# Four pairs of a tuned MoE kernel: inner product 2 split once more into seven small products

## The chip, the core and the metric

The kernel runs on one core of a Trainium2 chip. A core has five engines that each take their own instructions in order: TensorE (PE, matrix products; its weight loads are listed as PEld), VectorE (DVE), ScalarE (ACT), GpSimd (POOL), which here mostly issues DMAs, and SyncE (SP), which issues DMAs too. Engines wait for each other by semaphores. SBUF is the on-chip memory, PSUM the eight banks into which TensorE writes. The metric is the device time of one execution in microseconds (us); the median of the runs counts.

## The reference

A soft mixture of experts: every token goes through all eight experts, and the outputs are added, weighted by the softmax of the router's logits.

```python
# x: 16 x 512 x 512, router_logits: 16 x 512 x 8, expert_weights: 8 x 512 x 2048
probs = softmax(router_logits)
for e in range(8):
    output += probs[:, :, e:e+1] * (x @ expert_weights[e])
```

So the output is one product of a matrix of 8192 x 4096 (each token's x, scaled by each of its eight probabilities) with one of 4096 x 2048 (the experts' weights, stacked).

## The kernel before

The big product is done by a scheme of the Strassen-Winograd kind: a product of two matrices that are cut into 2 x 2 blocks is made of seven products of blocks in place of eight, at the price of sums of blocks. The first level gives seven outer products, numbered 1 to 7 here (P1 is the first). The second level cuts each again: each piece of it (a `Product`, 256 tokens by 1024 columns) is made of seven inner products, steps 1, 5, 6, 2, 7, 3, 4 (`STEPS`, L353), each of eight matmuls of 128x512 (`K8`). A `Left` holds the left operand of a piece in fp16: `t[0]`, `t[1]` (the two halves of its depth), and the sums `s2` and `i`; a `Right` holds the weights and their sums.

The pieces are run in pairs, called stages. P1 has stages 0 to 6 (`ND` = 7); its results are stored to the DRAM tensors `kept`. In a stage the two pieces take turns, step by step, in slots 0 to 13; the hooks (`at`) issue loads and other work ahead of a slot.

In stages 1 to 6 the first two steps, inner products 1 and 5 of both pieces, are split a third time (`by_thirds`, from L764 on). Both pieces have the same weights, so their two left operands stand above each other as a matrix of 256 tokens by 1024, which is cut into 2 x 2 blocks; the weights are cut likewise (`third_sums`, L178). Seven small products of four 128x256 matmuls each take the place of two full products of eight 128x512 matmuls each. The fourteen small products for steps 1 and 5 are listed in L778; (p, r) is small product r of inner product p. Their sums of left operands are made by `Thirds`.

Each small or full product leaves a result in a PSUM bank, and a copy by ScalarE or an add by VectorE takes it on:

- `bank()` (tile `ps`) has six buffers, `bank2()` (tile `pt`) two. `by_thirds` keeps both `pt` banks, one for inner product 1 and one for 5; products 1 and 4 of each go through it, and the last one, (5, 4), is copied out by ScalarE (L812).
- `Product.post_alone` (L591 on) is what follows a full step. After step 1 ScalarE copies the bank of product 1 into a second PSUM bank, `b` (L596), onto which step 2 adds its matmuls; the result is then copied to an SBUF tile `h` (L604) and stored. Steps 5 and 6 are copied to `h` (L600), and steps 7 and 3 add a bank to such an `h` on VectorE.
- `h` tiles (`hpool`, 12 buffers) hold the pieces' results until their store by POOL (L121) has landed, the four sums of `Thirds`, and a few others. A tile that needs a buffer waits until an older one is free.

The order on VectorE is the order in which the program issues its work. Work that isn't bound to a slot (a `Left`'s halves, `s2`, `i`, the sums of `Thirds`, sums of weights) is put into a first-in first-out queue with an assumed cost (`later`). `slack` (L384), called after each product, keeps two clocks, one of TensorE and one of VectorE, and issues tasks from that queue while VectorE's clock is behind TensorE's; `need` issues at once all that stands ahead of a task that a product is about to use. `evacuated` charges an add to VectorE's clock.

Besides, POOL loads and stores weights during P1: casts of the expert's weights at slots 8, 2, 0 and 9 of stages 1, 3 and 5, and the "wedge" in stages 2 to 3 and 4 to 5, three VectorE sums of weights at the start of stages 3 and 5.

Of the kernel before, what the change touches and what calls it, by code (L numbers as in the profile page):

```python
# [31 lines left out]
def kernel(  # L32
# [7 lines left out]
    nc = tc.nc  # L40
# [3 lines left out]
    ADD, SUB, MUL = mybir.AluOpType.add, mybir.AluOpType.subtract, mybir.AluOpType.mult  # L44
# [5 lines left out]
    C = H // P  # L50
# [4 lines left out]
    HQ = 256  # L55
# [21 lines left out]
    def half():  # L77
        return h_tile([P, NB], f32)
# [27 lines left out]
    def tt(o, a, b, op):  # L106
        dve(nc.vector.tensor_tensor(out=o, in0=a, in1=b, op=op))  # L107
# [15 lines left out]
    def bank():  # L123
        return psum.tile([P, NB], f32, name="ps", tag="ps")

    def bank2():
        return psum.tile([P, NB], f32, name="pt", tag="pt", bufs=2)

    def mm(ps, z, w, start, stop):
        note(nc.tensor.matmul(ps, z, w, start=start, stop=stop, skip_group_check=True))  # L130
# [9 lines left out]
    def new_z():  # L140
        return zpool.tile([P, K8, HQ], f16, name="z", tag="z")
# [217 lines left out]
    class Task:  # L359


        def __init__(self, cost, make):
            self.cost, self.make, self.done = cost, make, False
# [10 lines left out]
    def need(task):  # L374
        if task is not None and not task.done:
            flush(task)
            clock["pe"] = max(clock["pe"], clock["dve"])

    def later(cost, make, first=False):
        t = Task(cost, make)  # L380
        (queue.appendleft if first else queue.append)(t)
        return t

    def slack(slot=SLOT, lag=LAG):  # L384
        clock["dve"] = max(clock["dve"], clock["pe"])
        clock["pe"] += slot
        while queue and clock["dve"] < clock["pe"] - lag:
            queue.popleft().run()

    def evacuated(cost=0.69):  # L390
        clock["dve"] = max(clock["dve"], clock["pe"]) + cost
# [53 lines left out]
    class Left:  # L445
# [6 lines left out]
        def make(self, k):  # L452
            if self.of is not None:
                need(self.of.task[k])
            t = self.t[k] = new_z()
            times(t, k, self.xb, self.pb)
            if self.less is not None:
                u = new_u()
                times(u, k, *self.less)
                tt(t, t, u, SUB)  # L460
            if self.of is not None:
                tt(t, self.of.t[k], t, SUB)
            if self.kept is not None:
                tt(t, t, self.kept.t[:, ds(k * K8, K8), :], SUB)
# [19 lines left out]
        def op(self, p):  # L484
            need(self.task[{1: 0, 5: 0, 6: "s2", 2: 1, 4: 1, 3: "i", 7: "i"}[p]])
            if p == 6:
                return self.s2
            t, i = {1: (self.t[0], 0), 5: (self.t[0], 1), 2: (self.t[1], 0), 4: (self.t[1], 1),
                    3: (self.i, 0), 7: (self.i, 1)}[p]
            return t[:, :, ds(i * HP, HP)]  # L490
# [19 lines left out]
    class Thirds:  # L510
# [19 lines left out]
        def queue(self):  # L530
            self.a.queue_make(0)
            self.b.queue_make(0)
            self.task = later(2.76, self.make)
            for left in (self.a, self.b):
                left.queue_s2()
            for left in (self.a, self.b):
                left.queue_make(1)
# [7 lines left out]
    class Right:  # L545
# [15 lines left out]
        def op(self, p):  # L561
            need(self.task.get(p))
            return self.w[p]

    TN = {2: (0, 0), 3: (0, 1), 4: (1, 0), 7: (1, 1)}

    class Product:


        def __init__(self, right, left, sink, base=None, steps=STEPS):  # L570
            self.right, self.left, self.sink, self.base, self.steps = right, left, sink, base, steps
            self.loads, self.banks, self.o = [], {}, {}
            self.apart = False

        def step(self, p):
            b = "q" if p in (5, 3) else "b" if p == 2 else "x"
# [14 lines left out]

        def post_alone(self, p, x, q, b):
            o = self.o
            if p == 1:
                self.banks["b"] = bank()
                act(nc.scalar.copy(self.banks["b"], x))  # L596
            elif p in (5, 6):
                tn = (1, 1) if p == 5 else (0, 1)
                o[tn] = half()
                act(nc.scalar.copy(o[tn], q if p == 5 else x))  # L600
            elif p in (2, 4):
                if TN[p] not in o:
                    o[TN[p]] = half()
                act(nc.scalar.copy(o[TN[p]], b if p == 2 else x))  # L604
            else:
                evacuated()
                tt(o[TN[p]], x if p == 7 else q, o[TN[p]], ADD)

# [19 lines left out]
    ND = 7  # L628
# [28 lines left out]
    def at(stage, slot, make):  # L657
        hooks.setdefault((stage, slot), []).append(make)
# [105 lines left out]
    def by_thirds(stage):  # L764

        some = stages[stage]
        left = thirds[stage]
        cols = [ds(i * HQ, HQ) for i in range(2)]
        place, keep = {}, {}

        def at_once(what):
            if what not in place:
                t = place[what] = (bank2 if what[0] == "x" else bank)()
                if what[0] in "gh":
                    some["gh".index(what[0])].banks["x" if what[1] == 1 else "q"] = t
            return place[what]
        slot = 0
        for n, (p, r) in enumerate(((1, 1), (5, 1), (1, 5), (1, 6), (5, 6), (5, 5), (1, 2),  # L778
                                    (1, 7), (5, 7), (1, 3), (1, 4), (5, 2), (5, 3), (5, 4))):
            if n in (0, 4, 7, 11):  # L780
                for make in hooks.get((stage, slot), ()):
                    make()
                slot += 1
                if slot == 2:
                    queue_lefts(stage + 1)
                    start_loads(stage + 2)
            x = at_once(("x", p))[:, cols[0]]
            q = at_once("q")[:, cols[p // 5]] if n > 1 else None
            g = at_once(("g", p))
            if r == 1:  # L790
                keep[p] = half()
            o = q if r in (5, 3) else g[:, cols[0]] if r == 2 else x
            z, w = left.op(r, p // 5), left.weights[p][r]
            for c in range(C):
                mm(o, z[:, c, :], w[:, c, :], (r == 1 or (p, r) == (1, 5)) and c == 0, c == C - 1)
            slack(0.4375, LAG if n < 6 else 1.3)
            if r == 1:
                act(nc.scalar.copy(g[:, cols[0]], x))
            elif r == 5:
                act(nc.scalar.copy(keep[p][:, cols[1]], q))  # L800
            elif r == 6:
                act(nc.scalar.copy(keep[p][:, cols[0]], x))
            elif r == 7:
                evacuated(0.42)
                tt(at_once(("h", p))[:, cols[1]], x, keep[p][:, cols[1]], ADD)
            elif r == 3:
                evacuated(0.42)
                tt(g[:, cols[1]], q, keep[p][:, cols[0]], ADD)
                if p == 1:
                    some[0].post(1)  # L810
            elif r == 4:
                act(nc.scalar.copy(place["h", p][:, cols[0]], x))  # L812
                if p == 1:
                    some[1].post(1)
        for product in some:
            product.post(5)
        return 4

    def queue_lefts(stage):
        if stage in thirds:  # L820
            if thirds[stage].task is None:
                thirds[stage].queue()
        elif stage < len(stages):
            for p in stages[stage]:
                queue_left(p.left)

    def run(stage):
        some = stages[stage]
        for p in some:
            p.left.queue_i()  # L830
        n = by_thirds(stage) if stage in thirds else 0
        for i in range(n // 2, len(some[0].steps)):
            for p in some:
                for make in hooks.get((stage, n), ()):
                    make()
                p.step(p.steps[i])
                slack()
                p.post(p.steps[i])
                n += 1
                if n == wait_for.get(stage, 1):  # L840
                    queue_lefts(stage + 1)
                if n == late.get(stage, 1):
                    start_loads(stage + 2)
                if n == 5:
                    store_loads(stage + 1)
                if n == 7:
                    finish_loads(stage + 2)
# [283 lines left out]
    def third_at(stage, slot, of, r, p):  # L1131
        def make():
            of[p] = third_sums(right[r].w[p])
        at(stage, slot, lambda: later(2.76, make))
    third_at(ND, 5, third2, 2, 1)
    third_at(ND, 7, third2, 2, 5)
    third_at(k3, 3, third3, 3, 1)
# [96 lines left out]
```

## Time and profile before

| | us |
|---|---|
| median of three runs | 1361.7 (1361.27 to 1362.39) |
| the profiled run | 1360.91 |
| its span, first to last instruction | 1359.1 |
| one of stages 2 to 5 | 23.38 |

All times of the trace below are microseconds from the start of the span. In a timeline a line gives the start, the time from the first to the last of the merged instructions (the number of them stands after the x), the engine, the line of the program, the operation, what it writes from what it reads, the shapes, and in brackets the idle time of the engine before it with what ended it. In a group of instructions the numbers after the bar are the busy time, the mean duration of one in ns, and the idle time before them. Ends of matmuls are modelled: a matmul's listed duration is longer than the distance to the next one.

### The profile page before, as it was taken

What the parts mean: (1) busy time and instruction counts of PE and PEld (TensorE: products, weight loads), DVE (VectorE), ACT (ScalarE), POOL (GpSimd) and SP (SyncE); (2) the same over time, 40 slices, a digit from 0 to 9 for tenths busy, and PEclk for the clock granted to TensorE, in tenths of its full rate; (3) what the DMA queues carried; (4) which work ended last, traced back from release to release, by engine and by line L of the source; (5) the groups of instructions that cost most, each with busy time, mean ns of one, the idle gap of its engine ahead of it and who ended that gap; (6) DMA issues with size and microseconds to landing.
All of it is one profiled execution on the core that took longest, in us unless ns stands there. A gap on an engine that the chain in (4) does not pass through costs nothing.

```text
span 1359.1 us, 18757 instructions
## 1 busy us (share of the span) xinstructions
PE 1352.8 (100%) x6846; PEld 667.1 (49%) x6846; DVE 1133.7 (83%) x1374; ACT 261.4 (19%) x525; POOL 435.9 (32%) x667
## 2 busy tenths in 40 slices
PE   9999999999999999999999999999999999999998
PEld 4555555565544444444444444444444444556564
DVE  7877687878999888787887899988889897898884
ACT  3232423233211111111111100000000000224331
POOL 3223323333222332323312122453434443232342
PEclk9999999999999999999999999999999999999999
DMA  9899979888899999999997998999999999999997
GB/s 186 242 221 247 258 232 233 255 243 250 238 341 288 287 310 273 288 285 284 309 274 279 345 318 236 247 267 251 264 251 249 263 265 315 327 302 251 199 163 131
DMA packets 191116, 355.65 MB, mean 262 GB/s; under 512 B 53040, under 2 KB 81968, under 8 KB 186160
## 3 DMA queue, kind: packets, MB, share of 16 engines
q0 software_dynamic: 89824, 189.31, 59.6%
q1 hardware_dynamic: 97456, 139.86, 33.5%
q10 hardware_dynamic: 3744, 25.30, 4.7%
q8 instruction: 53, 0.87, 0.3%
q14 instruction: 39, 0.32, 0.1%
HBM read 210.53 MB, written 180.55 MB: 288 GB/s over the span
## 4 chain that ended last, share of the span: by engine, by line
PE 99%; DMA 0%; DVE 0%; issue 0%; POOL 0%; ACT 0%; POOLq 0%
PE ps L130 75%; PE pt L130 24%; DMA w<-in_x_dram 0%; DVE z L255 0%; POOL w L121 0%; DVE h L107 0%; ACT h L1180 0%; DVE lg L295 0%; POOLq L1218 0%
## 5 line engine op out<-in xcount | busy, mean ns | idle before, releaser
L130 PE MATMUL ps<-w,z 128*128 128x512 f16 (+1 forms) x3776 | 821.3, 374 | 0.0
L130 PEld LDWEIGHTS <-z 128*128 128x128 f16 x5264 | 515.0, 98 | 574.4
L121 POOL DMA_DIRECT2D out_dram<-h x380 | 256.7, 710 | 684.1 <-ACT h L617 269.5
L130 PE MATMUL pt<-w,z 128*128 128x512 f16 (+1 forms) x1488 | 312.7, 357 | 0.0
L107 DVE TENSOR_TENSOR z<-xT,pT 128x2048 f16<-128x2048 f16 x220 | 265.9, 1217 | 0.8 <-DMA xT<-xs 0.8
L107 DVE TENSOR_TENSOR h<-ps,h 128x512 f32<-128x512 f32 x250 | 170.2, 687 | 88.0 <-PE ps L130 67.2
L130 PE MATMUL ps<-w,d 128*128 128x512 f16 x880 | 199.1, 379 | 0.0
L604 ACT COPY h<-ps 128x512 f32<-128x512 f32 x118 | 69.2, 586 | 417.9 <-PE ps L130 385.3
L130 PEld LDWEIGHTS <-d 128*128 128x128 f16 x880 | 86.1, 98 | 99.8
L107 DVE TENSOR_TENSOR z<-z,d 128x2048 f16<-128x2048 f16 x110 | 131.8, 1216 | 0.0
L107 DVE TENSOR_TENSOR h<-pt,h 128x512 f32<-128x512 f32 x123 | 83.5, 686 | 43.3 <-PE pt L130 41.0
L107 DVE TENSOR_TENSOR w<-w 128x1024 f16<-128x1024 f16 (+2 forms) x104 | 110.2, 1075 | 1.9 <-PE ps L130 1.0
L617 ACT COPY h<-ps 128x512 f32<-128x512 f32 x50 | 29.3, 586 | 391.5 <-PE ps L130 387.1
L107 DVE TENSOR_TENSOR ps<-ps,h 128x512 f32<-128x512 f32 (+1 forms) x90 | 51.9, 579 | 28.5 <-PE ps L130 24.9
L107 DVE TENSOR_TENSOR d<-z 128x1024 f16<-128x1024 f16 x110 | 74.7, 684 | 1.1
L600 ACT COPY h<-ps 128x512 f32<-128x512 f32 x97 | 53.8, 604 | 69.4 <-PE ps L130 65.3
L121 POOL DMA_DIRECT2D kept<-h x56 | 30.6, 548 | 93.7 <-ACT h L604 52.6
L121 POOL DMA_DIRECT2D out_dram<-kept x56 | 56.9, 1058 | 11.2 <-DMA out_dram<-h 5.8
L596 ACT COPY ps<-ps 128x512 f32<-128x512 f32 x59 | 33.6, 570 | 120.7 <-PE ps L130 62.6
L107 DVE TENSOR_TENSOR ps<-pt,h 128x256 f32<-128x256 f32 x38 | 16.4, 432 | 41.5 <-PE pt L130 29.4
L107 DVE TENSOR_TENSOR h<-h 128x512 f32<-128x512 f32 (+2 forms) x69 | 45.1, 675 | 0.6 <-DMA out_dram<-h 0.4
L107 DVE TENSOR_TENSOR z<-z,u 128x2048 f16<-128x2048 f16 x36 | 44.1, 1225 | 1.2
(74 smaller groups left out, 558.6 us busy)
## 6 DMA issues: line engine op xcount, KB each, us to landing
out_dram<-h POOLq DMA_DIRECT2D x380, 256.0 KB, 7.5
pT<-p_dram SPq DMA_DIRECT2D x126, 256.0 KB, 7.7
w<-wd ACTq DMA_DIRECT2D x23, 1024.0 KB, 9.4
xT<-x SPq DMA_DIRECT2D x80, 256.0 KB, 7.7
h<-kept SPq DMA_DIRECT2D x72, 256.0 KB, 7.7
h<-out_dram SPq DMA_DIRECT2D x68, 256.0 KB, 6.7
w<-in_expert_weights_dram POOLq DMA_DIRECT2D x33, 512.0 KB, 10.3
kept<-h POOLq DMA_DIRECT2D x56, 256.0 KB, 6.0
```

The costliest lines, as they stand in the source:

```text
L107: dve(nc.vector.tensor_tensor(out=o, in0=a, in1=b, op=op))
L121: note(nc.gpsimd.dma_start(out=o, in_=i, **how))
L130: note(nc.tensor.matmul(ps, z, w, start=start, stop=stop, skip_group_check=True))
L596: act(nc.scalar.copy(self.banks["b"], x))
L600: act(nc.scalar.copy(o[tn], q if p == 5 else x))
L604: act(nc.scalar.copy(o[TN[p]], b if p == 2 else x))
L617: act(nc.scalar.copy(o[tn], b))
```

## The change

In stages 2 to 5, inner product 2 of the two pieces is split like 1 and 5. A class `Twos` makes the sums of the left operands: four VectorE sums of 128x512, in a new tile `z`, as one task with an assumed cost of 1.68 us. `by_twos` runs the fourth to ninth slot of such a stage: the seven small products 1, 5, 6, 2, 7, 3, 4 stand between the full steps 6 and 7 of the two pieces. The sums of product 2's weights are made once, in stage 1. The result of product 1 is copied to SBUF, into the piece's `h` for quarter (0, 0), instead of PSUM; when the small products are done, VectorE adds their result to it (`end`).

```diff
+    class Twos:
...
+        def make(self):
+            e0, e1 = ds(0, C), ds(C, C)
+            a, b = (left.t[1][:, :, ds(0, HP)] for left in (self.a, self.b))
+            t = new_z().rearrange("p (s c) (two t) -> p s c two t", s=2, two=2)
+            for i, (p, x, y, op) in enumerate(((5, b[:, e0], b[:, e1], ADD), (6, 5, a[:, e0], SUB),
+                                               (3, a[:, e1], 6, SUB), (7, a[:, e0], b[:, e0], SUB))):
+                self.s[p] = t[:, i // 2, :, i % 2]
+                tt(self.s[p], *(self.s[v] if isinstance(v, int) else v for v in (x, y)), op)
+        def queue(self):
+            self.task = later(1.68, self.make)
+        def op(self, r):
+            need(self.task)
+            if r in self.s:
+                return self.s[r]
+            left = self.b if r == 4 else self.a
+            return left.op(2)[:, ds(0 if r == 1 else C, C), :]
...
         def post_alone(self, p, x, q, b):
             o = self.o
-            if p == 1:
+            if p == 1 and self.two:
+                o[0, 0] = half()
+                act(nc.scalar.copy(o[0, 0], x))
+            elif p == 1:
                 self.banks["b"] = bank()
                 act(nc.scalar.copy(self.banks["b"], x))
...
+    def by_twos(stage):
+
+        some, of = stages[stage], twos[stage]
+        c0, c1 = (ds(i * HQ, HQ) for i in range(2))
+        x, q, g, h = bank2(), bank2(), bank(), bank()
+        keep = []
+
+        def small(r):
+            o = q if r in (5, 3) else g if r == 2 else x
+            o = o[:, c1 if o is q else c0]
+            z, w = of.op(r), of.weights[2][r]
+            for c in range(C):
+                mm(o, z[:, c, :], w[:, c, :], r in (1, 5) and c == 0, c == C - 1)
+            slack(0.4375)
+            if r == 1:
+                act(nc.scalar.copy(g[:, c0], x[:, c0]))
+            elif r == 5:
+                keep.append(half())
+                act(nc.scalar.copy(keep[0][:, c1], q[:, c1]))
+            elif r == 6:
+                act(nc.scalar.copy(keep[0][:, c0], x[:, c0]))
+            elif r == 7:
+                evacuated(0.42)
+                tt(h[:, c1], x[:, c0], keep[0][:, c1], ADD)
+            elif r == 3:
+                evacuated(0.42)
+                tt(g[:, c1], q[:, c1], keep[0][:, c0], ADD)
+                end(0, g)
+            elif r == 4:
+                act(nc.scalar.copy(h[:, c0], x[:, c0]))
+                end(1, h)
+
+        def end(i, of):
+            o = some[i].o[0, 0]
+            evacuated()
+            tt(o, of, o, ADD)
+            some[i].sink((0, 0), o)
+
+        def full(i, p):
+            some[i].step(p)
+            slack()
+            some[i].post(p)
+        for slot, todo in enumerate((((1,), (5,)), ((0, 6),), ((6,), (2,)), ((1, 6), (7,), (3,)), ((0, 7),), ((4,), (1, 7))), 4):
+            for make in hooks.get((stage, slot), ()):
+                make()
+            for what in todo:
+                (small if len(what) == 1 else full)(*what)
+            if slot + 1 == 5:
+                store_loads(stage + 1)
+            if slot + 1 == 7:
+                finish_loads(stage + 2)
+        return 10
...
     def run(stage):
         some = stages[stage]
+        if stage in twos:
+            twos[stage].queue()
         for p in some:
             p.left.queue_i()
         n = by_thirds(stage) if stage in thirds else 0
+        if stage in twos:
+            n = by_twos(stage)
...
+    third_at(1, 5, third, 1, 2)
+    for stage in range(2, ND - 1):
+        twos[stage] = Twos(*(p.left for p in stages[stage]), third)
+        for p in stages[stage]:
+            p.two = True
```

The program as built has 64 fewer matmuls of 128x512 and 112 more of 128x256; VectorE has 16 sums of 128x512 (fp16), 8 adds of 128x256, 8 of 128x512 and 4 weight sums of 128x1024 more; ScalarE has 16 copies of 128x256 more and 8 of 128x512 fewer. The DMAs are the same ones.

More of the change, by code (lines that the diff above doesn't have):

```diff
@@ L563, in op, with __init__ @@
             return self.w[p]
+    class Twos:
+        def __init__(self, a, b, weights):
+            self.a, self.b, self.weights, self.s, self.task = a, b, weights, {}, None
+        def make(self):
[14 more added lines that the diff above has]
+            return left.op(2)[:, ds(0 if r == 1 else C, C), :]
     TN = {2: (0, 0), 3: (0, 1), 4: (1, 0), 7: (1, 1)}
@@ L572, in __init__ @@
             self.loads, self.banks, self.o = [], {}, {}
-            self.apart = False
+            self.apart = self.two = False
         def step(self, p):
@@ L817, in by_thirds @@
         return 4
+    twos = {}
+    def by_twos(stage):
[46 more added lines that the diff above has]
+        return 10
     def queue_lefts(stage):
```

## The prediction

> **What bounds the kernel now.** I read the page first, then the waits of TensorE, then the stretches of the four changed stages.
>
> ```profile
> span 1359.1 us, 18757 instructions
> PE 1352.8 (100%) x6846; PEld 667.1 (49%) x6846; DVE 1133.7 (83%) x1374; ACT 261.4 (19%) x525; POOL 435.9 (32%) x667
> PE 99%; DMA 0%; DVE 0%; issue 0%; POOL 0%; ACT 0%; POOLq 0%
> ```
> ```profile
> PE every L89 <- DVE h L86: 1.3, 1, 1.3
> PE ps L130 <- DMA w<-in_x_dram: 0.4, 1, 0.4
> PE ps L130 <- DVE lg L295: 0.3, 1, 0.3
> ```
> ```profile
> 87.65:111.03 23.38, 23.38 (x137) 13.33 (x136) 15.11 (x20) 8.23 (x18) 7.31 (x12) 1.00 1.17 263
> 111.03:134.41 23.38, 23.38 (x137) 13.29 (x136) 17.22 (x22) 8.23 (x18) 8.92 (x15) 1.00 1.10 255
> 134.41:157.79 23.38, 23.38 (x137) 13.33 (x136) 16.38 (x22) 8.24 (x18) 7.33 (x12) 1.00 1.12 233
> 157.79:181.17 23.38, 23.38 (x137) 13.29 (x136) 17.61 (x23) 8.23 (x18) 8.52 (x15) 1.00 1.08 305
> ```
>
> TensorE is the chain (99%), and all its waits are three at the kernel's start. Of the stretches (columns: PE, PEld, DVE, ACT, POOL busy, clock, DMA share, GB/s) each is one of stages 2 to 5; S below is a stage's start. Each lasts 23.38 us with TensorE busy in all of it, so time is won only by giving TensorE fewer columns, and lost by every wait put before it. VectorE is busy 15.1 to 17.6 us of 23.38.
>
> **The change part by part: TensorE's gain.**
>
> ```profile
> 92.89 0.60 PE L130 MATMUL ps<-w,h 128*128 128x256 f16 x4
> 93.33 0.60 PE L130 MATMUL pt<-w,z 128*128 128x256 f16 x4
> 93.77 3.62 PE L130 MATMUL ps<-w,d 128*128 128x512 f16 x16
> 97.22 13.98 PE L130 MATMUL ps<-w,z 128*128 128x512 f16 x64
> 111.03 1.04 PE L130 MATMUL pt<-w,z 128*128 128x256 f16 x8
> ```
>
> From 97.22 to 111.03 are 64 full matmuls: 0.2158 us each, 1.727 for a product of eight. A small product of four 128x256 matmuls takes 0.437 (87.65 to 93.77 is 14 of them). Per stage the two full products 2 (3.453) become seven small ones (3.06): -0.39, over four stages -1.57 us. That is the most this change can gain, 0.12%.
>
> **The wait before small product 5.** The new code takes both two-buffer banks of by_thirds (pt) at once. Small 1 gets the one free early; small 5 gets the one that the last small product of by_thirds, (5,4), has just filled and ScalarE must copy out first. Only small 1 stands between.
>
> ```profile
> 92.74 0.57 ACT L596 COPY ps<-ps 128x512 f32<-128x512 f32 x1 [1.90 <-DVE ps L107]
> 93.23 0.36 ACT L812 COPY ps<-pt 128x256 f32<-128x256 f32 x1
> 94.05 0.57 ACT L596 COPY ps<-ps 128x512 f32<-128x512 f32 x1 [0.46 <-DVE ps L107]
> 94.53 0.36 ACT L812 COPY ps<-pt 128x256 f32<-128x256 f32 x1
> 94.80 1.59 ACT L600 COPY h<-ps 128x512 f32<-128x512 f32 x3
> 97.42 0.59 ACT L600 COPY h<-ps 128x512 f32<-128x512 f32 x1 [1.03 <-PE ps L130]
> ```
> ```profile
> 0.96 0.27 DVE L86 MEMSET h<- 128x256 uint32 x1
> 1.29 4.45 PE L89 MATMUL every<-h 128*128 128x512 f16 x10 [1.29 <-DVE h L86]
> ```
>
> ScalarE works in order. Its copy of product 1 now goes to SBUF and no longer waits for a PSUM bank as at 94.05. Start to start a 512 copy takes 0.50 (three in 1.59 of 0.59 each), a 256 copy 0.27 (94.53 to 94.80): copies at 92.74, 93.24, 93.51, and that of (5,4) at 94.01, which also is when its data are there (93.33+0.60, and ScalarE starts 0.03 after a product's end: 93.77+3.62 to 97.42). It ends at 94.37. TensorE starts 0.06 after its releaser (0.96+0.27 to 1.29): 94.43, instead of 93.77+0.437=94.21. Stall 0.22 per stage, +0.88 in four. Bounds per stage: 0.17 with ScalarE free sooner, 0.35 with a tenth more at two hand-overs.
>
> **VectorE's added work.** Per stage: four sums of 128x512 f16 for the small products, two adds of 128x256 in PSUM, two ends of 128x512. Once, in stage 1, the four weight sums of product 2.
>
> ```profile
> L107 DVE TENSOR_TENSOR z<-z,d 128x2048 f16<-128x2048 f16 x110 | 131.8, 1216 | 0.0
> L107 DVE TENSOR_TENSOR w<-w 128x1024 f16<-128x1024 f16 x68 | 45.2, 685 | 0.6
> L107 DVE TENSOR_TENSOR ps<-pt,h 128x256 f32<-128x256 f32 x38 | 16.4, 432 | 41.5 <-PE pt L130 29.4 <-ACT h L800 12.0
> L107 DVE TENSOR_TENSOR h<-ps,h 128x512 f32<-128x512 f32 x250 | 170.2, 687 | 88.0 <-PE ps L130 67.2 <-issue 13.9 <-DMA out_dram<-h 3.0
> ```
>
> A 128x512 f16 sum has no row. From 2048 to 1024 elements the time falls 0.531, so 512 gives 0.685-0.266=0.42 (my estimate); bounds 0.34 (half of 1024's) and 0.685 (no gain at all). Added: 4x0.42+2x0.43+2x0.69=3.9 us per stage, on 15.1 to 17.6: it fits into 23.0, so what counts is where in VectorE's queue it stands. The weight sums (4x0.685) lie in stage 1 among posts whose banks TensorE needs only two products (3.45 us) later: hidden.
> [...]
>
> In stages 2, 3 and 5 the built program puts these four sums ahead of by_thirds' own adds, into time in which VectorE waits for TensorE. In stage 4 they come behind them, since the planner thinks VectorE busy after the wedge tasks of stage 3; then follow both i, both next lefts and the four thirds of the next stage, and only then the add of small product 7, whose bank small 4 overwrites.
>
> ```profile
> 70.49 1.22 DVE L107 TENSOR_TENSOR z<-z,d 128x2048 f16<-128x2048 f16 x1
> 71.62 2.35 DVE L107 TENSOR_TENSOR z<-xT,pT 128x2048 f16<-128x2048 f16 x2
> ...
> 138.18 0.87 DVE L107 TENSOR_TENSOR ps<-pt,h 128x256 f32<-128x256 f32 x2 [2.49 <-PE pt L130]
> ...
> 140.29 0.43 DVE L107 TENSOR_TENSOR ps<-ps,h 128x256 f32<-128x256 f32 x1 [0.88 <-PE ps L130]
> 140.63 2.35 DVE L107 TENSOR_TENSOR z<-xT,pT 128x2048 f16<-128x2048 f16 x2
> 143.02 0.69 DVE L107 TENSOR_TENSOR h<-z 128x1024 f16<-128x1024 f16 x1
> 143.75 0.69 DVE L107 TENSOR_TENSOR h<-h,z 128x1024 f16<-128x1024 f16 x1
> 144.47 0.69 DVE L107 TENSOR_TENSOR h<-z,h 128x1024 f16<-128x1024 f16 x1
> 145.08 0.69 DVE L107 TENSOR_TENSOR h<-z 128x1024 f16<-128x1024 f16 x1
> 145.68 1.29 DVE L107 TENSOR_TENSOR d<-z 128x1024 f16<-128x1024 f16 x2
> ```
>
> The last by_thirds add frees VectorE at 140.63-134.41=S+6.22. A dependent op starts 0.04 after the end of the one before (143.02 to 143.75), an independent one 0.08 before it (144.47 to 145.08): the four sums take 2x0.46+2x0.34=1.60 (S+7.82), two i 2x1.13 (70.49 to 71.62; S+10.08), two lefts 2.39 (140.63 to 143.02; S+12.47), thirds 2.66 (143.02 to 145.68; S+15.13), the add 0.43, the hand-over 0.06: small 4 may start at S+15.62. TensorE is there after 14 and six small products and three full ones, 20x0.437+3x1.727=13.92, plus 0.22: S+14.14. Stall 1.48. Bounds: 0 if the sums slip into VectorE's idle 2.49 us before 138.18, which the program's order excludes; 2.5 with sums of 0.685. In the three other stages the same add stands at S+6.22+1.13+2.39+2.66=S+12.40 or earlier (a wedge there puts one left and the thirds behind it), so TensorE finds it done.
>
> Adds of later products, the stores' issues on POOL (same number, issued later in the stage since half (0,0) is finished later) and the loads on SP keep their order and have VectorE's or the queue's idle time as cover; ScalarE gets 4 short copies more per stage and 2 long ones fewer, at 8.2 us of 23.38.
>
> **Sum.** -1.57+0.88+1.48=+0.8: a span of 1359.9. The profiled run took 1360.91, 1.8 above its span, and lies 0.8 below the median of the runs, 1361.7. Predicted median 1362.5.
>
> **The rivals.** *One stall less* (stage 4's is hidden, or small 5 finds its bank free): 1361.0 or 1361.6; without both 1360.1. For it: VectorE idles 2.49 us before 138.18. Against: engines take their instructions in order.
>
> *Stores hold the buffers: slower.* Product 1's two halves and one kept half now occupy three of the twelve h buffers from about S+5 on.
>
> ```profile
> DMA to landing us min/median/max: 2.5/7.3/14.2
> ```
> ```profile
> 109.51 0.59 ACT L604 COPY h<-ps 128x512 f32<-128x512 f32 x1 [8.05 <-PE ps L130]
> ```
> ```profile
> 190.11 1.84 ACT L600 COPY h<-ps 128x512 f32<-128x512 f32 x3 [1.18 <-DMA kept<-h]
> ```
>
> These stores (60 to 190 us) land late behind weight casts, and before the change one already held ScalarE 1.18 us. The new keep copy (small 5) needs, by the order of the stores, a buffer whose store follows ScalarE's last copy but one of the stage before, issued from S-0.9 on (109.51+0.59 against 111.03). Behind it on ScalarE are a 512 copy and the copy that small 7 waits for: 0.27+0.50+0.37+0.06=1.2. Small 7 is due at S+6.12+0.22+4x0.437+2x1.727=S+11.54, so this decides from a landing of 11.2 us on. At 14.2 it costs 3.0 in one stage: 1365.5. Against: the median is 7.3 and the casts stand behind such stores in most stages.
>
> *The clock drops.* The ten matmuls at 1.29 took 4.45 us, about 0.45 each, twice the later 0.2158, so a half-speed state exists. If one of five stalls brought about as long a spell (4 us, of which half is lost), +2 each, all five +10: 1364.5 to 1372. Against: 1.00 in every stretch, and the stalls are short. [...]
>
> **How the numbers follow.** Forecast 0.66, one stall less 0.15, stores 0.15, clock 0.04. 0.2% (2.7 us) is about what a measurement of this kernel can tell from no change. Faster by that much would need more than the largest gain of 1.57: 0.02, for errors between sessions. Slower: stores, clock and a little of the forecast's tail, 0.20. Same: 0.78. Range 1360.5 (no stage-4 stall, 0.17 each for small 5, and 0.4 of scatter) to 1365.3 (sums of 0.685 and 0.35 per small 5, a late store in part).
>
> **What would show it.** In the four stretches: 28 matmuls of 128x256 in place of 16 full ones; TensorE idle about 0.2 us before small 5, released by ScalarE's copy of (5,4); in stage 4 alone about 1.5 us before small 4, released by VectorE's add; stages 2, 3, 5 of some 23.2 us, stage 4 of 24.7; sums of about 0.42. It is wrong if small 5 doesn't wait, if stage 4's stall is missing or stands in other stages too, or if ScalarE waits for a kept store for over a microsecond.

## The result, and the profile after

The changed kernel takes 1364.62 us (median of 22 runs; the kernel before beside it 1362.26, also 22): a ratio of 1.0025, 95% interval 1.0016 to 1.0035. The forecast, 1362.5 against 1361.7, was a ratio of 1.0006, too little to tell from no change; measured, the kernel is slower, and the interval lies clear of 1. The two medians alone differ by 0.17%; the ratio also weighs six runs of 1368 to 1372 us (see the clock, below). One of the 22 runs took 1779.7 us at a mean granted clock of 0.752 and is not in the ratio.

The page of the profiled run (1364.85 us) shows it at once: TensorE's share of the chain that ended last fell from 99% to 92%, and DMAs, which had none of it, have 4%.

```profile
span 1363.1 us, 18914 instructions
PE 1351.7 (99%) x6894; PEld 671.4 (49%) x6894; DVE 1149.9 (84%) x1410; ACT 261.8 (19%) x533; POOL 436.0 (32%) x667
PE 92%; DMA 4%; DVE 2%; issue 1%; POOL 0%; ACT 0%; DVEq 0%; POOLq 0%; ACTq 0%; SPq 0%
```

TensorE's waits by engine and line, after (total, times, longest): three are new in the changed stages.

```profile
PE ps L130 <- ACT h L828: 2.2, 1, 2.2
PE pt L130 <- DVE ps L107: 1.2, 1, 1.2
PE pt L130 <- ACT ps L840: 0.3, 1, 0.3
```

The stretches of stages 2 to 5, after (columns as before: PE, PEld, DVE, ACT, POOL busy, clock, DMA share, GB/s):

```profile
87.91:111.40 23.49, 23.19 (x149) 14.44 (x148) 17.94 (x28) 8.39 (x20) 7.32 (x12) 1.00 1.10 261
111.40:134.67 23.27, 23.14 (x149) 14.49 (x148) 19.07 (x27) 8.39 (x20) 8.92 (x15) 1.00 1.13 241
134.67:161.65 26.98, 23.46 (x149) 14.48 (x148) 20.29 (x31) 8.19 (x20) 7.33 (x12) 1.00 1.12 246
161.65:184.92 23.27, 23.14 (x149) 14.45 (x148) 20.20 (x30) 8.39 (x20) 9.06 (x15) 1.00 1.07 276
```

Three stages are 0.11 us shorter or longer than the 23.38 of before; stage 4 is 3.6 us longer. Together the four last 97.01 in place of 93.52: +3.49 of the +4.0 of the span (the rest: first loads at the kernel's start +0.26, and a wait of 0.33 at 798 us). The profiled run before lies 1.35 below the median of those 22, the one after 0.2 above its own; so +4.0 between the profiles is +2.4 between the medians.

TensorE's timeline after has the three waits with their places. From here on "late" is the distance from one matmul's start to the next, less the usual 0.2158 (512 columns) or 0.1093 (256); the idle time in brackets is some 0.16 smaller, since the listed ends of matmuls overlap.

```profile
94.97 0.60 PE L130 MATMUL pt<-w,z 128*128 128x256 f16 x4 [0.30 <-ACT ps L840]
...
135.98 1.04 PE L130 MATMUL pt<-w,h 128*128 128x256 f16 x8
139.17 0.60 PE L130 MATMUL ps<-w,h 128*128 128x256 f16 x4 [2.15 <-ACT h L828]
...
152.59 0.60 PE L130 MATMUL pt<-w,z 128*128 128x256 f16 x4 [1.24 <-DVE ps L107]
```

- 94.97 is small product 5 of stage 2, late by 0.46 (in stages 3 to 5 by 0.29 each, too short to be listed).
- 152.59 is small product 4 of stage 4, late by 1.40. It was forecast.
- 139.17 is not one of the new products: it is (5, 5) of `by_thirds`, at the start of stage 4, late by 2.31. It waits for ScalarE's keep copy at L828, and ScalarE's timeline says for what that one waited:

```profile
93.17 0.59 ACT L621 COPY h<-ps 128x512 f32<-128x512 f32 x1 [2.06 <-DMA kept<-h]
...
138.75 0.37 ACT L828 COPY h<-ps 128x256 f32<-128x256 f32 x1 [2.64 <-DMA kept<-h]
```

Both wait for an `h` buffer that a store to `kept` still reads. The stall at 93.17 mostly hid (0.17 of it reached small product 5). That at 138.75 did not: with it -1.57 (TensorE's gain) +1.33 (small 5: 0.46+3x0.29) +1.40 +2.31 = +3.47, against the +3.49 measured.

The first store of stage 3, in POOL's timeline of before and then of after:

```profile
123.41 0.55 POOL L121 DMA_DIRECT2D kept<-h  x1 [1.72 <-ACT h L604]
```
```profile
125.60 0.55 POOL L121 DMA_DIRECT2D kept<-h  x1 [2.40 <-DVE h L107]
```

and its DMA (KB, us from issue to landing), before and after:

```profile
kept<-h POOLq DMA_DIRECT2D x1, 256.0 KB, 8.6
```
```profile
kept<-h POOLq DMA_DIRECT2D x1, 256.0 KB, 13.1
```

Half (0, 0) of a piece is now finished by VectorE's `end`, after seven small products, and no longer by ScalarE's copy after step 2. So the store goes out 2.2 us later, and it took 4.5 us longer besides: it landed at 138.67, just before the copy at 138.75 (before: at 132.00). The later issue alone would have cost nothing: with the 8.6 of before the store would have landed at 134.2, and ScalarE wanted the buffer at 136.1 (138.75 less the 2.64 of waiting).

### The profile page after: what moved, and what is told of

The parts are those of the page before. It is cut to its first block, busy times and chain, and to the rows that moved or that the text cites. A ratio compares the mean times of both kernels' runs of the same rounds, so it can differ in the third digit from the quotient of the medians.

```text
span 1363.1 us, 18914 instructions
## 1 busy us (share of the span) xinstructions
PE 1351.7 (99%) x6894; PEld 671.4 (49%) x6894; DVE 1149.9 (84%) x1410; ACT 261.8 (19%) x533; POOL 436.0 (32%) x667
## 4 chain that ended last, share of the span: by engine, by line
PE 92%; DMA 4%; DVE 2%; issue 1%; POOL 0%; ACT 0%; DVEq 0%; POOLq 0%; ACTq 0%; SPq 0%
PE ps L130 69%; PE pt L130 23%; DMA kept<-h 2%; DMA h<-out_dram 1%; DVE z L107 1%; DMA w<-in_expert_weights_dram 1%; DVE h L107 1%; DMA pT<-p_dram 0%; DVE w L107 0%; DVE ps L107 0%; DVE u L107 0%; POOL w L121 0%; POOL wd L121 0%; ACT ps L840 0%; ACT h L621 0%
## 5 line engine op out<-in xcount | busy, mean ns | idle before, releaser
L130 PE MATMUL ps<-w,z 128*128 128x512 f16 (+1 forms) x3728 | 810.7, 374 | 0.2 <-DVE z L107 0.2
L130 PE MATMUL pt<-w,z 128*128 128x512 f16 (+1 forms) x1584 | 325.9, 352 | 2.4 <-DVE ps L107 1.2
L107 DVE TENSOR_TENSOR h<-ps,h 128x512 f32<-128x512 f32 x258 | 175.3, 687 | 80.1 <-PE ps L130 62.5
L632 ACT COPY h<-ps 128x512 f32<-128x512 f32 x110 | 64.5, 587 | 402.2 <-PE ps L130 359.6
L645 ACT COPY h<-ps 128x512 f32<-128x512 f32 x50 | 29.3, 586 | 392.9 <-PE ps L130 369.9
L628 ACT COPY h<-ps 128x512 f32<-128x512 f32 x97 | 53.9, 601 | 75.6 <-PE ps L130 75.6
L624 ACT COPY ps<-ps 128x512 f32<-128x512 f32 x51 | 29.1, 570 | 111.2 <-PE ps L130 62.6
L107 DVE TENSOR_TENSOR ps<-pt,h 128x256 f32<-128x256 f32 x46 | 19.8, 432 | 36.3 <-PE pt L130 29.8
L107 DVE TENSOR_TENSOR z<-z 128x2048 f16<-128x2048 f16 (+1 forms) x48 | 45.6, 957 | 1.4
## 6 DMA issues: line engine op xcount, KB each, us to landing
w<-in_expert_weights_dram POOLq DMA_DIRECT2D x33, 512.0 KB, 10.1
```

What stands on the lines that cost most here:

```text
L645: act(nc.scalar.copy(o[tn], b))
```

## Experiments

All ratios are to the kernel before, measured in the same session. e1 to e4 and e8 vary one part each or all, e5 asks which `h` tile matters, e6 and e7 combine, e9 to e12 go after the stores.

**e1: the sums first.** The four sums are issued at once, in all four stages, ahead of by_thirds' adds.

```diff
     twos[stage].queue()
+    flush(twos[stage].task)
```

> The small products' sums (and all that stands ahead of them in VectorE's queue) are issued at a stage's start, so in stage 4 they fall into VectorE's idle time before by_thirds' own adds. Theory (three separate waits add up: 4 x 0.29 us before small 5, 1.24 before small 4 of stage 4, 2.15 at stage 4's start behind a kept store): the 1.24 goes, the other two stay; TensorE's idle time in stage 4 falls from 3.7 to about 2.5 us, the median from about 2.4 us over the kernel before to about 1.2 over it. Rival (VectorE has too little time in stages 3 and 4, and the wait only moves): another VectorE wait of about 1 us appears in stage 4 or 5, and the median stays.

Ratio 1.0009 (0.9998 to 1.002). Stages 23.30, 23.27, 24.42, 23.27. Small 4 no longer waits: VectorE's order was its cause. The wait for L828 at the start of stage 4 stays, at 1.16 late; stage 3's first store landed at 137.10 here.

```profile
137.60 0.60 PE L130 MATMUL ps<-w,h 128*128 128x256 f16 x4 [0.99 <-ACT h L828]
```

**e2: small product 5 later,** behind full step 6 of the first piece.

```diff
-enumerate((((1,), (5,)), ((0, 6),), ((6,), (2,)), ...
+enumerate((((1,),), ((0, 6), (5,)), ((6,), (2,)), ...
```

> Small 5 stands behind the full step (0,6) instead of ahead of it. Theory: its bank has long been copied out, so the 0.29 us before it go in each of the four stages, 1.16 us in all; the waits in stage 4 stay, the median falls by about 1.2. Rival (ScalarE is late as such): small 6, small 3 or small 7 waits for the copy of small 5 or 6 instead, 0.2 to 0.4 us per stage, and the median stays.

Ratio 1.0025 (1.0013 to 1.0036). Stages 2 and 3 take 22.99 and 22.98, which is the full gain: the bank's copy-out was what small 5 waited for. Stages 4 and 5 take 25.35 and 24.68: the wait for the buffer now stands at the start of both (0.68 and 1.70 late), and small 4 of stage 4 is 1.69 late. So the median doesn't fall by the 1.2 that was expected, and stays 2.8 over the kernel before:

```profile
136.55 0.60 PE L130 MATMUL ps<-w,h 128*128 128x256 f16 x4 [0.52 <-ACT h L828]
149.97 0.60 PE L130 MATMUL pt<-w,z 128*128 128x256 f16 x4 [1.53 <-DVE ps L107]
162.92 0.60 PE L130 MATMUL ps<-w,h 128*128 128x256 f16 x4 [1.54 <-ACT h L828]
```

The stores' landings differ too. Stage 3's first store landed at 136.05, 2.6 earlier than in the kernel after; stage 4's, issued at 151.27, took 11.2 us, where the one of the kernel after, issued at 153.89, took 4.3. Whether the earlier issue made it late is not shown.

**e3: thirteen `h` buffers.** The room for the thirteenth comes from another pool, that of `d` and `s2` (three to two).

```diff
-spool = ... bufs=3
+spool = ... bufs=2
...
-hpool = ... bufs=12
+hpool = ... bufs=13
```

> A thirteenth h buffer (the room comes from the third s2 buffer). Theory: ScalarE's copy at stage 4's start (L828) no longer needs the buffer of the kept store that landed at 138.7, so TensorE's wait of 2.15 us is gone, and with it the runs of 1368 to 1372 us with a granted clock of 0.997 to 0.998, if these are executions in which that wait was longer; median about 0.2 over the kernel before. Rival 1 (another resource held ScalarE): the wait stays at 2 us. Rival 2 (the clock falls for another reason, such as the many short waits): the runs of 1368 and more stay. Two s2 buffers could make VectorE's s2 wait for step 6 of the other piece; in the groups of VectorE this would show as idle time before d.

The buffer wait at the start of stage 4 falls to 0.20, although the store took 12.4 us and landed at 137.97; the 1.24 at small 4 stays, as it should.

```profile
138.47 0.60 PE L130 MATMUL pt<-w,h 128*128 128x256 f16 x4 [0.20 <-ACT h L830]
```

The whole is slower all the same, 1.0075 (1.006 to 1.0091): with two buffers VectorE can't make the next `d` until TensorE has read the last but one, a wait that neither the kernel before nor the one after has, and TensorE then waits for VectorE after stage 6. Among the waits of this kernel, VectorE's and then TensorE's:

```profile
DVE d L107 <- PE ps L130: 47.3, 25, 2.8
```
```profile
PE ps L130 <- DVE ps L107: 3.9, 3, 2.6
PE ps L130 <- DVE h L107: 3.1, 9, 0.4
```

**e4: e1, e2 and e3 together.**

> All three edits together. Theory: the waits are independent and all go; stages 2 to 5 last 22.99 us each, the span is 1.57 us under that of the kernel before, ratio 0.9988. Rival (the waits cover each other or VectorE is the bound): the gain is less than 0.8 us and TensorE shows new waits in stages 2 to 5.

Stages 22.99, 22.98, 23.09, 22.98: 92.04, so 1.48 us less than before, without a wait. That is the forecast's gain of 1.57, all but 0.09. The ratio is 1.0042 (1.003 to 1.0054), from the same later waits as in e3.

**e5: the kept half in `d`'s pool,** so that only product 1's halves are added to `h`.

```diff
-keep.append(half())
+keep.append(spool.tile([P, NB], f32, name="d", tag="d"))
```

> As the changed kernel, but the half that small products 5 and 6 leave (keep) lies in the third s2 buffer, which is free then, in place of an h buffer; nothing else is touched. Theory (the twelve h buffers are one too few while late stores hold them): ScalarE's waits on kept stores at the starts of stages 4 and 5 fall below 0.5 us and TensorE's with them; small 5 (0.29 to 0.5 us per stage) and small 4 of stage 4 (1.4) still wait; median about 1 us over the kernel before, and runs of 1368 us and more are gone. Rival (the late store itself, not the number of buffers, is what counts: ScalarE simply needs the next one): the wait at stage 4's start stays near 2 us.

Ratio 1.002 (1.0011 to 1.0029), stage 4 26.52: the wait for L828 falls only from 2.31 to 1.85 late. So the kept half alone isn't the main thing; what is left is product 1's two halves and the late store, which e9 takes up. Small 5 of stage 2 is late by 0.29 here instead of 0.46, so 0.17 of it did come from the buffers.

**e6: e1 and e2, twelve buffers.**

> Sums first and small 5 later together, twelve h buffers. Theory: only the wait on the kept store is left, some 0.5 to 2.3 us and varying from run to run; stages 2 to 5 last 92.0 us plus that wait; median between 0.8 us under and 0.8 us over the kernel before. Rival (without its other waits TensorE runs earlier and meets the store later, so the wait grows by what was taken away): the sum of stages 2 to 5 stays near 94.3 us, as with the sums first alone.

Ratio 1.0002 (0.9994 to 1.0011). Stages 22.98, 22.99, 23.07, 24.46: one wait is left, 1.48 late at the start of stage 5. It eats the gain of four stages nearly to the hundredth (93.50 against 93.52).

```profile
160.13 0.60 PE L130 MATMUL ps<-w,h 128*128 128x256 f16 x4 [1.31 <-ACT h L828]
```

**e7: e6 with e5's edit.**

> Sums first, small 5 later, and keep in the s2 buffer. Theory: no wait in stages 2 to 5, 92.0 us for the four, nothing lost later since the s2 pool keeps three buffers: median 1.0 to 1.6 us under the kernel before. Rival: a new wait in stages 2 to 5, and no gain beyond 0.3 us.

Ratio 1.0002 (0.9994 to 1.0011); the one wait is 1.16 late in place of 1.48.

**e8: eleven `h` buffers,** otherwise the kernel after.

> The changed kernel with eleven h buffers: the suspected cost doubled. Theory: ScalarE meets late stores in more places and for longer; TensorE waits 2 us or more in at least two of stages 2 to 6, the median rises by 3 us or more over the changed kernel, and more runs show a granted clock under 0.999. Rival (the buffers are not short): under 1 us more.

Ratio 1.0079 (1.0062 to 1.0097). Stage 2 now takes 24.86 and stage 4 29.53, and stage 6 waits too (1.75 late), while small 4's 1.24 doesn't change. One wait is over 2 us, where two were expected. The longest is put down to a copy at L826; the copy ahead of it on ScalarE, at L632, had waited 4.54 us for a store to `kept`.

```profile
93.11 0.60 PE L130 MATMUL pt<-w,h 128*128 128x256 f16 x4 [1.44 <-ACT h L830]
140.66 1.41 PE L130 MATMUL pt<-w,h 128*128 128x256 f16 x8 [3.04 <-ACT ps L826]
156.61 0.60 PE L130 MATMUL pt<-w,z 128*128 128x256 f16 x4 [1.24 <-DVE ps L107]
```

11, 12 and 13 buffers give 3.04, 2.15 and 0.20 of idle time at the start of stage 4, while the first store of stage 3 landed 3.5, 4.0 and 3.4 us into that stage. So the number of buffers counts by itself.

**e9: two casts elsewhere.** The casts of weight block (0, 1) move from stage 3, slot 2, to stage 4, slot 12; otherwise the kernel after.

```diff
-((1, 8), (3, 2), (5, 0), (5, 9))
+((1, 8), (4, 12), (5, 0), (5, 9))
```

> The kernel after, but the two weight casts of stage 3 (slot 2) are issued in stage 4, slot 12. Theory (stage 3's first stores land late because they stand behind these two casts in POOL's queue): stage 3's first store lands about 4 to 8 us after its issue instead of 13.07, ScalarE's keep copy L828 at the start of stage 4 doesn't wait, and stage 4 loses the 2.31 us there and keeps 1.40 at small product 4: 24.7 in place of 26.98; the ratio falls by about 0.0017, to some 1.0008. The casts now stand ahead of stage 5's stores, so a wait may come up later than stage 5. Rival (the stores are late because of all the traffic of the stage, the wedge's stores and the loads on SP): the landing takes over 10 us again and at least half of the 2.31 us stays.

Ratio 1.0011 (1.0002 to 1.002), stages 23.26, 23.27, 24.67, 23.31. The store issued at 125.81 lands in a third of the time, the wait at the start of stage 4 is gone, and 1.24 at small 4 is all that is left there beside small 5's 0.29. (Its profiled run, 1367.3, is the slowest of the eleven; two waits for VectorE around 1150 us are 3.2 of it.)

```profile
kept<-h POOLq DMA_DIRECT2D x1, 256.0 KB, 4.4
```
```profile
150.49 0.60 PE L130 MATMUL pt<-w,z 128*128 128x256 f16 x4 [1.24 <-DVE ps L107]
```

So the two casts made the store late. By which way they did is less clear. DMAs in another queue were late too: the transposes that SP issues between 118 and 122.9, after and then in e9, with POOL's stores of the wedge beside them:

```profile
wd<-w POOLq DMA_DIRECT2D x2, 512.0 KB, 10.1
xT<-xs SPq DMA_TRANSPOSE x3, 15.1
```
```profile
wd<-w POOLq DMA_DIRECT2D x2, 512.0 KB, 5.1
xT<-xs SPq DMA_TRANSPOSE x4, 4.1
```

The casts themselves, in the kernel after (issued between 114.4 and 115.3):

```profile
w<-in_expert_weights_dram POOLq DMA_DIRECT2D x2, 512.0 KB, 10.1
```

So with the casts there the other queue's DMAs took 15.1 us against 4.1, and POOL's own 10.1 against 5.1 (the store 13.1 against 4.4). Whether the store was late by its place behind the casts in POOL's queue, or as the other queue's DMAs were, was not separated.

The casts are not the whole of it. The kernel before issued the same two casts at the same place, and its store took 8.6 us. Over all traces in which they stand there, this store took between 7.7 (e6) and 13.1 us (the kernel after); with them moved away and no others in their place, 4.4, 4.3 and 4.1 (e9, e11, e12). What sets it between 7.7 and 13.1 stays open, and so the 2.31 us are the size of the wait in one execution.

**e10: e6 with the casts swapped:** those of the wedge go from stage 4, slot 2, to stage 3, slot 2, and those of block (0, 1) from there to stage 4, slot 12.

> Both edits of e6 (Twos' sums issued first, small product 5 after product 6) with 12 h buffers, and the wedge casts of stage 4, slot 2 issued in stage 3, slot 2, where the other two casts stood, and those in stage 4, slot 12. Theory (the one wait left in e6, 1.48 us at the start of stage 5, is the store of stage 4 behind the wedge casts): stage 4's first store lands within 8 us instead of 10.93, no wait of TensorE is left in stages 2 to 5, each lasts about 23.0, 92.0 in all, and the kernel is 1.5 us faster than before: ratio about 0.999. Rival (the queue carries the same bytes, so the wait only goes to another stage): stages 2 to 6 still lose 1 to 2 us somewhere, ratio 1.000 or above.

The wait at the start of stage 5 is gone, as the theory had it, and one at the start of stage 4 has come: stage 3's first store, now behind the wedge's casts, takes 12.9 us.

```profile
kept<-h POOLq DMA_DIRECT2D x1, 256.0 KB, 12.9
```

The ratio is 1.0002 (0.9993 to 1.0011). The rival was right that the wait only moves. In its profile stage 4 took 26.93: 2.19 late, and some 1.7 more for a reason not named so far. It is TensorE's clock; here are the stretches around the wait:

```profile
137.00:138.00 1.00, 0.00 (x0) 0.00 (x0) 0.00 (x0) 0.22 (x1) 0.02 (x1) 1.00 1.79 180
138.00:138.80 0.80, 0.60 (x6) 0.54 (x6) 0.00 (x0) 0.79 (x3) 0.70 (x1) 0.99 0.45 107
138.80:142.20 3.40, 3.40 (x18) 2.42 (x17) 0.93 (x3) 0.37 (x1) 0.74 (x1) 0.50 1.00 320
142.20:143.00 0.80, 0.80 (x9) 0.72 (x8) 0.36 (x1) 0.40 (x1) 0.00 (x0) 1.00 1.11 257
```

After 2.03 us of idleness TensorE ran 3.4 us at half clock: 1.7 us lost. In e8 the 3.04 us before 140.66 were followed by the same:

```profile
141.20:144.40 3.20, 3.20 (x17) 2.21 (x15) 0.00 (x0) 1.12 (x3) 1.81 (x3) 0.50 0.98 294
```

**e11: e6 with e9's move,** the wedge's casts left where they were.

> Both edits of e6 and the two casts of e9 moved from stage 3, slot 2, to stage 4, slot 12; the wedge casts stay in stage 4, slot 2. Theory (a stage's first stores are late by the casts ahead of them in POOL's queue): stage 3's stores land within 5 us, so the queue is empty when the wedge casts of stage 4 come, these are done some 3 us earlier than in e6 (153.51), stage 4's first store lands before 157 instead of 159.63, and of e6's 1.48 us at the start of stage 5 less than 0.5 is left: stages 2 to 5 together 92.0 to 92.5, ratio 0.999 to 0.9995. Rival (the wedge casts alone make stage 4's stores late, whatever stood ahead of them): the first store of stage 4 lands at 159 or later again, and 1 us or more stays at the start of stage 5; ratio 1.0002.

The best of all: 1361.29 against 1362.14, ratio 0.9993 (0.9985 to 1.0002). Stages 22.98, 22.98, 23.09, 22.98, 92.03 in all. The first store of stage 4 lands in 3.1 us, at 155.1, where e6's took 10.9:

```profile
kept<-h POOLq DMA_DIRECT2D x1, 256.0 KB, 3.1
```

The first wait for `h` comes in stage 6 now, 0.75 late. The gain is as large as forecast for TensorE alone, and still within what can be told from no change. Its profiled run, 1363.89, is the slowest of the eleven and shows where such a gain goes: the start took 3.08 us longer (first loads, and a spell at half clock, see the last section), and two waits for VectorE at 786 and 797 us, which the kernel before doesn't have, cost 0.88.

**e12: e11 with the wedge's casts two slots earlier.**

> e11 with the wedge casts of stage 4 issued two slots earlier (slot 0, some 2 us, ahead of the two xs loads). Theory: the casts land 1 to 2 us earlier than in e11, no wait of TensorE is left in stages 2 to 5, each lasts about 23.0; ratio about 0.999, 1.4 us faster than before. Rival: the casts take the DMA engines when stage 3's last stores and the loads of lefts need them, and stage 4's or 5's start waits for these; ratio 1.000 or above.

Ratio 1.0016 (1.0006 to 1.0025), a miss. The profile shows 92.52 for the stages (0.48 late in stage 5 for ScalarE) and can't explain 2 us of median; three of its 12 runs had a mean clock of 0.997 to 0.998.

## Why the prediction was wrong

*The bound, and TensorE's gain: right.* -0.39 a stage; without waits e4 and e11 show -1.48 and -1.49 in four, against -1.57 forecast.

*The wait before small 5: right, mis-sized.* 0.22 a stage was forecast, within 0.17 to 0.35; 0.29 was measured in three stages, since ScalarE's copy of (5, 4) is 0.38 long (0.36 was used) and starts 0.05 later than worked out. Stage 2's 0.46 holds 0.17 from a store. e2 shows the cause.

*The sums: right.* All sixteen, VectorE's group by shape after:

```profile
L107 DVE TENSOR_TENSOR z<-z 128x512 f16<-128x512 f16 x16 | 6.4, 422 | 0.3
```

0.42 was the estimate, from the rows of 2048 and 1024 elements; 0.422 was measured.

*Stage 4's stall at small 4: right,* in place, cause (e1) and size: 1.48 forecast, 1.40 measured. VectorE's queue after shows the order that was counted through:

```profile
143.20 1.67 DVE L107 TENSOR_TENSOR z<-z 128x512 f16<-128x512 f16 x4
144.79 2.35 DVE L107 TENSOR_TENSOR z<-z,d 128x2048 f16<-128x2048 f16 x2
147.06 2.35 DVE L107 TENSOR_TENSOR z<-xT,pT 128x2048 f16<-128x2048 f16 x2
...
152.11 0.76 DVE L107 TENSOR_TENSOR ps<-pt,h 128x256 f32<-128x256 f32 x2
```

Since by_thirds itself was 2.31 late, VectorE was as late as TensorE, and the stall stood behind the other in full; e9, where by_thirds was not late, shows the same 1.41.

*The step that failed:* "the stores' issues on POOL (same number, issued later in the stage since half (0,0) is finished later) ... have VectorE's or the queue's idle time as cover". It saw the later issue and costed it at nothing. The cover was a free `h` buffer, and three of twelve had just been taken. e3, e8 and e9 show it from both ends: with one more buffer 0.37 of the 2.31 us is left, with an earlier landing nothing, and with one buffer less it is 3.20. That one term is most of the 2.7 us by which the sum missed (+0.8 for +3.5); small 5 is the other 0.45. How long the store would take, 13.1 in place of 8.6, no row of before could tell.

*The rival "Stores hold the buffers"* had the mechanism, and its mark ("ScalarE waits for a kept store for over a microsecond") came true with 2.64 and 2.06. It had 0.15, and it looked for the wait at one place, the new keep copy of small 5. The copies of `by_thirds` at the next stage's start (L828) take buffers from the same stores, have hardly any slack (TensorE is at (5, 5) five small products, 2.2 us, into the stage), and come while even the first store of the stage before may be on its way. "The median is 7.3" spoke against it, but the stores that matter are those behind casts: 13.1. The prediction has the casts behind such stores in most stages; in stage 3 they stand ahead (before: casts issued from 114.10 on, the store at 123.41).

*The rival "The clock drops"* had 0.04, and the profile of the kernel after doesn't show it: its idle 2.15 us went by at clock 1.00, and so did what followed; why, when e10's 2.03 did not, is not shown. Yet six of its other 21 runs took 1368.1 to 1371.6 with a mean clock of 0.997 to 0.998. In the sessions of the experiments one of 96 runs of the kernel before went to 0.998. That the stalls bring spells like e10's in these runs is likely, but argued: none of the six was profiled. One spell (3.4 us at half clock, 1.7 lost, of 1363) lowers the mean clock by 0.0012, so 0.002 to 0.003 would be two; two cost 3.4 us, and the six runs are 4 to 8 us above the median of the other fifteen, so this isn't all. It matters for the ratio: the mean of all 21 runs is 3.5 us above that of the kernel before, the mean of the fifteen 1.8. So the waits that are shown above account for the profiled run, and about half of the measured slowdown comes from runs whose cause stays open.

## What to carry to other kernels

When a change makes a result later, follow its store to the landing, and ask which later instructions take buffers from that pool; ask it of every user of the pool, the unchanged ones first, and use the landing of the stores at that place, not the median. Where an engine is 99% of the chain, one wait undoes a gain of 0.1% (1.48 us in e6 against 1.57): remove the waits one by one, and expect the next late thing to show up a stage later (at the start of stage 5 in e6, of stage 6 in e11). Casts of weights are best issued where no store that somebody waits for is on the way: here the first store of stage 3 took 8.6 (before) and 13.1 us (after) with them ahead of it, and 4.4 with them moved (e9).

## What was not expected of the hardware

After some two microseconds without matmuls TensorE ran at half clock for 3.4 us in some traces and at full clock in others. In e11 the half clock came at the kernel's start, after 1.66 us and some shorter gaps before it (TensorE's timeline; two matmuls of 512 columns take 0.85 instead of 0.43 from start to start until 15 us):

```profile
11.21 0.76 PE L130 MATMUL pt<-w,z 128*128 128x512 f16 x2 [1.66 <-DMA w<-in_expert_weights_dram]
11.76 1.06 PE L130 MATMUL ps<-w,z 128*128 128x512 f16 x2
12.62 1.06 PE L130 MATMUL pt<-w,z 128*128 128x512 f16 x2
```

These are the waits of TensorE of 1.66 us and more in all traces, with the granted clock after them (for e3 and e9 in stretches of 50 and 25 us, in which e10's spell shows as 0.97 and 0.93):

| run | the wait, us | clock after it |
|---|---|---|
| e8 | 3.04, up to 140.66 | 0.50 from 141.2 to 144.6 |
| e3 | 2.6, for VectorE | 1.00 |
| e9 | 2.2, for VectorE | 1.00 |
| after | 2.15, up to 139.17 | 1.00 |
| e10 | 2.03, up to 138.20 | 0.50 from 138.8 to 142.2 |
| e5 | 1.69, up to 138.47 | 1.00 |
| e11 | 1.66, up to 11.21 | 0.50 from 11.5 to 14.9 |

So the length of the wait alone doesn't say which it will be: 1.66 us were followed by half clock, 2.6 were not. What else decides is not shown. A stall of about 2 us cost nothing more in the kernel after, and 1.7 us more in e10.
